# k loaded as plain float32 and rounded on chip by VectorE and GpSimd in turns, outputs planned nine slots behind instead of ten

## The chip, the cores and the metric

One core of one Trainium2 chip runs the whole problem. The metric is device time in microseconds (us), the median of several runs. The profile is one further execution, recorded by the hardware profiler; its span runs from the first to the last instruction of the core.

## The reference, cut to what matters

The inputs are `k` and `v`, each 16 x 2048 x 256 float32 (33.55 MB each), and two vectors `w` and `u` of 256. The output has the shape of `v`. For each batch row and each of the 256 channels a recurrence runs over 2048 time steps:

```python
for t in range(seq_len):
    ww = u + k[b, t]
    qq = max(pp, ww); e1 = exp(pp - qq); e2 = exp(ww - qq)
    out[b, t] = (e1 * aa + e2 * v[b, t]) / (e1 * bb + e2 + 1e-08)
    ww = pp - w + k[b, t]
    qq = max(ww, k[b, t]); e1 = exp(ww - qq); e2 = exp(k[b, t] - qq)
    aa = e1 * aa + e2 * v[b, t];  bb = e1 * bb + e2;  pp = qq
```

So each output is a quotient of two sums over the past with exponentially decaying weights: a numerator with v and a denominator without.

## The kernel before, in words

Time is cut into 16 chunks of 128 steps, and the 16 batch rows into groups of four. One group of one chunk is a slot, n = 0 to 63, and four slots make a chunk (c = n // 4). A tile of k or v for one slot is 128 time steps (on the partitions) x 4 batch rows x 256 channels, 512 KB. In each slot:

- `load_k` and `load_v` bring the two tiles in. For slots 0 to 3 SP issues them (lines 81 and 88), later GpSimd (POOL in the profile; lines 84 and 88). The tile that TensorE multiplies is of type float32r. POOL's load of k has a float32r tile as its target, so the transfer itself converts; SP's loads bring float32 into buffers of v's pool, and `round_k` (VectorE, line 168) copies them into float32r tiles, for the first four slots alone.
- `logs` (TensorE, lines 174 and 177) turns k into two sets of exponents by matrix products, in two PSUM tiles X that are shared with the denominators.
- `exps` (ScalarE, line 181, called ACT) writes their exponentials to the ring `EZR`, which holds 12 slots.
- `cast_v` (line 185) makes a bf16 copy `vb` of v, on VectorE for slots 0 to 9 and on POOL after that; there are two `vb` buffers. `times_v` (VectorE, called DVE, line 190) multiplies it into the ring.
- `sums` (TensorE, line 217) adds up the chunk's totals. After the fourth slot of a chunk a chain of small steps (VectorE lines 223 to 286, two ACT steps at lines 240 and 259, two TensorE steps at lines 230 and 281) computes what the chunk inherits from all earlier ones, and `inject` (four SP transfers of 8 KB, line 295) writes that into the ring.
- `den` and `num` (TensorE, line 307), `log_den` and `inverse` (ACT, lines 316 and 320: a logarithm and an exponential that make the reciprocal), `mult` (VectorE, line 328) and `store` (SP, three transfers at lines 334 and 337) make the output. `num` has one PSUM buffer, the output tile `ot` three buffers, so the product of slot n waits until the store of slot n - 3 has landed.

The order of all this is made by a planner at the end of the kernel. Each piece is a step with an engine, a cost, steps that it must follow, a due time, and a buffer that it takes or gives back. The planner runs these through a list scheduler with a slot of 3.9 us and prints each engine's instructions in the order it finds; on the chip each engine works through its list in that order and waits where an input or a buffer isn't ready. The due time of the output steps of slot n is LAG = 10 slots after that of its exponentials. Where the plan leaves TensorE idle, `zeros` (line 114) inserts multiplications of zeros. Below, a step is named with its slot or chunk: RK for `round_k`, CV for `cast_v`, TV for `times_v`, X for `exps`, LN and INV for the two ACT steps of the output, MUL for `mult`, ST for `store`, IN for `inject`, FR for the first VectorE step of the chain behind line 240.

There are eight buffers of k (`kpool`, NK) and eight of v (`vpool`, NV). A buffer of k comes free when `logs` has read it.

Of the kernel before, what the change touches and what calls it, by code (L numbers as in the profile page):

```python
# [7 lines left out]
F32 = mybir.dt.float32  # L8
F32R = mybir.dt.float32r
# [6 lines left out]
def kernel(  # L16
# [9 lines left out]
    K = tc.keep_in_program_order  # L26
    PE, DVE, SC, POOL, SP = nc.tensor, nc.vector, nc.scalar, nc.gpsimd, nc.sync

    B, T, Dm = k.shape
# [3 lines left out]
    D = 2 * Dm  # L33
    NP = 4 * NST
    RING = 12
    LAG = 10
    BYSP = 4
    EARLY = 10
    NK, NV, NVB, NRD, NOT = 8, 8, 2, 2, 3
    RS = 2.0 ** -20  # L40
    CAP = 54.0
    BIG = 1e30
    SLOT = 3.9
# [2 lines left out]

    consts = ctx.enter_context(tc.tile_pool(name="consts", bufs=1))
    kpool = ctx.enter_context(tc.tile_pool(name="kpool", bufs=NK))
    vpool = ctx.enter_context(tc.tile_pool(name="vpool", bufs=NV))
    vbpool = ctx.enter_context(tc.tile_pool(name="vbpool", bufs=NVB))  # L50
    rpool = ctx.enter_context(tc.tile_pool(name="rpool", bufs=NRD))
# [20 lines left out]
    def rows_of(x, n):  # L72
        c, p = divmod(n, 4)
        return x[4 * p:4 * p + 4, c * TC:(c + 1) * TC, :].rearrange("n t d -> t n d")

    KR, VR, VB = {}, {}, {}

    def load_k(n):
        if n < BYSP:
            KR[n] = vpool.tile([128, 4, Dm], F32, tag="vr", name="kf")  # L80
            K(SP.dma_start(out=KR[n], in_=rows_of(k, n)))
        else:
            KR[n] = kpool.tile([128, 4, Dm], F32R, tag="kr", name="kr")
            K(POOL.dma_start(out=KR[n], in_=rows_of(k, n)))  # L84

    def load_v(n):
        vr = vpool.tile([128, 4, Dm], F32, tag="vr", name="vr")
# [5 lines left out]
    def rows_wu(x, g0):  # L93
        K(POOL.dma_start(out=WU[g0::64, :, :], in_=bass.AP(
            tensor=x.tensor, offset=x.offset, ap=[[0, 2], [0, 2], list(x.ap[0])])))

    load_k(0)
    K(SC.preload_act_table_set("natural_log_exp_and_others"))
    Z = consts.tile([128, 192], BF16, tag="Z", name="Z")
# [63 lines left out]

    X = [psx.tile([128, 2, D], F32, tag=f"X{a}", name=f"X{a}") for a in range(2)]

    def round_k(n):
        kr = kpool.tile([128, 4, Dm], F32R, tag="kr", name="kr")
        K(DVE.tensor_copy(kr, KR[n]))
        KR[n] = kr

    def logs(n, q, a):
        km = KR[n].rearrange("p (i n) d -> p i (n d)", i=2)
        for i in range(2):
            K(PE.matmul(X[a][:, i, :], (NLE, NLZ)[q], km[:, i, :], start=True, stop=False, skip_group_check=True))  # L174
        for i in range(2):
            g = 64 * i
            K(PE.matmul(X[a][:, i, :], CO[g:g + 64, q, :], WU[g:g + 64].rearrange("p n d -> p (n d)"),  # L177
                        start=False, stop=True, tile_position=(g, 0), skip_group_check=True))
# [121 lines left out]
    RD, NUM, OT = {}, {}, {}  # L300
# [42 lines left out]
    def step(name, eng, cost, fn, args=(), after=(), behind=(), due=0.0, port=False, take=None, give=(), move=None):  # L343
        ops[name] = dict(eng=eng, cost=cost, fn=fn, args=args, after=after, behind=behind, due=due, port=port,
                         take=take, give=give, move=move)

    for n in range(NP):
        c = n // 4
        t = SLOT * n
        e = LAG * SLOT  # L350
        last = SLOT * (4 * c + 3)
        early = n < BYSP
        q = "SP" if early else "POOL"
        qc = 0.6 if early else 0.76
        if n:
            step(("LK", n), q, qc, load_k, (n,), behind=[("LK", n - 1)], due=t - 14 * SLOT, take=("V", -1 - n) if early else ("K", n), move=0.524)
            step(("LV", n), q, qc, load_v, (n,), behind=[("LV", n - 1)], due=t - 9 * SLOT, take=("V", n), move=0.524)
        else:
            step(("LK", n), "-", 0.0, None, take=("V", -1 - n), move=0.524)
            step(("LV", n), q, qc, load_v, (n,), take=("V", n), move=0.524)  # L360
        if early:
            step(("RK", n), "DVE", 0.65, round_k, (n,), [("LK", n)], due=t - 2 * SLOT, port=True, take=("K", n),
                 give=[("V", -1 - n)])
        src = ("RK", n) if early else ("LK", n)
        for j in range(2):
            step(("L", j, n), "PE", 0.95, logs, (n, j), [src], [("L", 1 - j, n - 1 + j)], t - 1.5 * SLOT, take=("X", (j, n)),
                 give=[("K", n)] if j else [])
            step(("X", j, n), "ACT", 0.91, exps, (n, j), [("L", j, n), ("NUM", n - RING), ("S", n - RING)],
                 [("X", 1 - j, n - 1 + j)], t, give=[("X", (j, n))])
        step(("CV", n), "DVE" if n < EARLY else "POOL", 0.63 if n < EARLY else 1.0, cast_v, (n,), [("LV", n)],  # L370
             [("CV", n - 1)], t, True, ("VB", n), [("V", n)])
        step(("TV", n), "DVE", 1.14, times_v, (n,), [("X", 1, n), ("CV", n)], [("TV", n - 1)], t + 2 * SLOT, True,
             None, [("VB", n)])
        step(("S", n), "PE", 0.34, sums, (n,), [("TV", n)] + ([("CS", c - 1)] if n % 4 == 0 else []), [("S", n - 1)],
             t + 3 * SLOT)
        if n % 4 == 3:
            chain = (("CS", "DVE", 0.34, copy_sums, ("S", n)), ("TU", "PE", 0.45, turn, ("CS", c), ("BK", c - 1)),
                     ("CT", "DVE", 0.27, copy_turn, ("TU", c)), ("SL", "ACT", 0.23, state_logs, ("CT", c)),
                     ("FR", "DVE", 0.53, state_frames, ("SL", c), ("SN", c - 1)),
                     ("OF", "DVE", 0.39, state_offsets, ("FR", c)), ("SW", "ACT", 0.26, state_weights, ("OF", c)),  # L380
                     ("CH", "DVE", 0.95, state_chain, ("SW", c), ("KP", c - 1)),
                     ("SS", "DVE", 0.36, state_spread, ("CH", c)), ("TK", "PE", 0.23, turn_back, ("SS", c)),
                     ("BK", "DVE", 0.2, copy_back, ("TK", c)))
            for name, eng, cost, fn, *after in chain:
                step((name, c), eng, cost, fn, (c,), after, due=last + 1)
            step(("IN", c), "SP", 2.4, inject, (c,), [("BK", c)], due=last - 9, move=0.0)
            if c + 1 < NST:
                step(("SN", c), "DVE", 0.12, state_next, (c,), [("OF", c)], due=last + 2 * SLOT)
                step(("KP", c), "DVE", 0.12, state_keep, (c,), [("CH", c)], due=last + 2 * SLOT)
        step(("DEN", n), "PE", 0.44, den, (n,), [("IN", c)], [("DEN", n - 1)], t + e, take=("X", ("d", n)))  # L390
        step(("LN", n), "ACT", 0.92, log_den, (n,), [("DEN", n)], [("INV", n - 1)], t + e, take=("RD", n),
             give=[("X", ("d", n))])
        step(("INV", n), "ACT", 0.95, inverse, (n,), [("LN", n)], due=t + e)
        step(("NUM", n), "PE", 0.44, num, (n,), [("IN", c), ("TV", n)], [("NUM", n - 1)], t + e + 1, take=("N", n))
        step(("MUL", n), "DVE", 1.14, mult, (n,), [("NUM", n), ("INV", n)], [("MUL", n - 1)], t + e + 2, take=("OT", n),
             give=[("N", n), ("RD", n)])
        step(("ST", n), "SP", 1.8, store, (n,), [("MUL", n)], due=t + e + 4, move=0.524)
        step(("SD", n), "-", 0.0, None, after=[("ST", n)], give=[("OT", n)])
# [8 lines left out]
        elif name[0] in ("DEN", "NUM", "TK"):  # L407
            ops[name]["after"].append("mats")

    free = {"K": NK, "V": NV, "X": 2, "N": 1, "RD": NRD, "OT": NOT, "VB": NVB}  # L410
    free = {x: [(0.0, j) for j in range(m)] for x, m in free.items()}
    at = {"POOL": 5.6, "SP": 1.3, "ACT": 5.0, "DVE": 5.4, "PE": 6.0, "-": 0.0}
    need, users = {}, {}
# [7 lines left out]
    held, port, hbm, out_end = {}, 0.0, 0.0, 0.0  # L421
    while ready:
        best = {}
        for name, t in ready.items():
            o = ops[name]
            t = max(t, at[o["eng"]], port if o["port"] else 0.0)
            if o["take"]:
                if not free[o["take"][0]]:
                    continue
                t = max(t, min(free[o["take"][0]])[0])  # L430
# [5 lines left out]
        t, _, name = min(pick, key=lambda x: x[:2])  # L436
# [5 lines left out]
        if o["port"]:  # L442
            port = end
# [65 lines left out]
```

## Time and profile before

| | |
|---|---|
| runs without profile | 315.66 us median of 3 (315.4 to 323.72) |
| the profiled execution | 318.16 us, of which its span is 316.4 us |
| mean granted TensorE clock | 0.984 |
| busy | PE 284.3, ACT 259.6, DVE 235.7, POOL 158.6 us |
| moved by DMA | 101.66 MB, of it 67.12 MB read from HBM and 33.55 MB written |

PE's busy time holds 43.1 us of the multiplications of zeros. The loads of k and v go through two queues: q1 (issued by SP, and the stores too) and q0 (issued by POOL). Start times of single steps, as "X 16 starts at 67.4 us", are read from the timeline of the engine; the n-th instruction of a group belongs to slot n (X has two instructions for each slot).

### The profile page before, as it was taken

What the parts mean: (1) busy time and instruction counts of PE and PEld (TensorE: products, weight loads), DVE (VectorE), ACT (ScalarE), POOL (GpSimd) and SP (SyncE); (2) the same over time, 40 slices, a digit from 0 to 9 for tenths busy, and PEclk for the clock granted to TensorE, in tenths of its full rate; (3) what the DMA queues carried; (4) which work ended last, traced back from release to release, by engine and by line L of the source; (5) the groups of instructions that cost most, each with busy time, mean ns of one, the idle gap of its engine ahead of it and who ended that gap; (6) DMA issues with size and microseconds to landing.
All of it is one profiled execution on the core that took longest, in us unless ns stands there. A gap on an engine that the chain in (4) does not pass through costs nothing.

```text
span 316.4 us, 6751 instructions
## 1 busy us (share of the span) xinstructions
PE 284.3 (90%) x2524; PEld 134.0 (42%) x2524; DVE 235.7 (74%) x388; ACT 259.6 (82%) x289; POOL 158.6 (50%) x204
## 2 busy tenths in 40 slices
PE   7999797989797989888998989998998999999991
PEld 6444343434343434333443434434343444446560
DVE  5843869999877997686869687776859696978443
ACT  1776567979797989788897989988897999999880
POOL 7738564976287548664663656455564322200000
PEclk9999599999999999999999999999999999999997
DMA  7999999999999999999999999999999954448477
GB/s 242 358 387 400 399 398 391 370 358 365 377 292 368 366 371 355 369 337 374 383 313 385 338 375 344 323 364 365 388 318 383 317 161 138 134 119 241 130 238 218
DMA packets 83586, 101.66 MB, mean 321 GB/s; under 512 B 8280, under 2 KB 75872, under 8 KB 83552
## 3 DMA queue, kind: packets, MB, share of 16 engines
q0 software_dynamic: 40416, 62.93, 64.8%
q1 hardware_dynamic: 43136, 38.29, 39.2%
q8 instruction: 20, 0.33, 0.4%
q14 instruction: 14, 0.11, 0.1%
HBM read 67.12 MB, written 33.55 MB: 318 GB/s over the span
## 4 chain that ended last, share of the span: by engine, by line
DMA 35%; DVE 24%; PE 19%; SPq 8%; ACT 8%; issue 4%; DVEq 0%; POOL 0%
DMA out_dram<-ot 26%; DMA vr<-in_v_dram 7%; PE X L174 6%; DVE ot L328 6%; DVE AB L266 5%; DVE EZR L190 4%; PE X L177 4%; ACT rd L316 3%; ACT rd L320 3%; PE X L307 3%; SPq L337 3%; SPq L295 2%; PE num L307 2%; SPq L334 2%; DMA EZR<-cb 2%
## 5 line engine op out<-in xcount | busy, mean ns | idle before, releaser
L181 ACT ACTIVATE EZR<-X 128x1024 bf16<-128x1024 f32 x128 | 125.2, 1014 | 21.3 <-PE X L177 20.4
L328 DVE TENSOR_TENSOR ot<-num,rd 128x1024 f32<-128x1024 f32 x64 | 78.5, 1227 | 43.3 <-DMA out_dram<-ot 21.7
L185 POOL CAST vb<-vr 128x1024 bf16<-128x1024 f32 x54 | 61.1, 1131 | 69.1 <-DVE EZR L190 69.1
L190 DVE TENSOR_TENSOR EZR<-EZR,vb 128x2048 bf16<-128x2048 bf16 x64 | 79.3, 1248 | 11.4 <-ACT EZR L181 8.7
L316 ACT ACTIVATE rd<-X 128x1024 f32<-128x1024 f32 x64 | 65.5, 1023 | 13.7 <-PE X L307 11.6
L320 ACT ACTIVATE rd<-rd 128x1024 f32<-128x1024 f32 x64 | 67.6, 1056 | 1.6
L177 PE MATMUL X<-WU,CO 64*128 64x512 f32 x256 | 64.2, 498 | 1.4 <-DMA WU<-in_u_dram 1.4
L84 POOL DMA_DIRECT2D kr<-in_k_dram x60 | 46.5, 775 | 30.1 <-PE X L174 23.2
L88 POOL DMA_DIRECT2D vr<-in_v_dram x60 | 45.3, 755 | 15.5 <-issue 5.3
L174 PE MATMUL X<-kr,NLZ 128*128 128x512 f32 x128 | 47.3, 451 | 0.0
L174 PE MATMUL X<-kr,NLE 128*128 128x512 f32 x128 | 47.1, 449 | 0.0
L114 PE MATMUL TURN<-Z 128*128 128x192 bf16 x348 | 43.1, 260 | 3.2 <-DVE cb L286 2.1
L177 PEld LDWEIGHTS X<-WU,CO 64*128 64x128 f32 x256 | 24.1, 184 | 48.8 <-issue 47.0
L114 PEld LDWEIGHTS <-Z 128*128 128x128 bf16 x348 | 28.8, 103 | 19.9 <-issue 18.5
L307 PE MATMUL num<-EZR,LN 64*64 64x512 bf16 x256 | 25.6, 389 | 8.1 <-DVE ot L328 7.5
L217 PE MATMUL TOT<-EZR,OH 128*32 128x256 bf16 x512 | 26.7, 281 | 3.2 <-DVE EZR L190 3.2
L174 PEld LDWEIGHTS X<-kr,NLE 128*128 128x128 f32 x128 | 19.3, 191 | 17.9 <-issue 8.5
L307 PE MATMUL X<-EZR,L 64*64 64x512 bf16 x256 | 26.2, 398 | 0.3
L174 PEld LDWEIGHTS X<-kr,NLZ 128*128 128x128 f32 x128 | 19.3, 190 | 16.8 <-issue 12.3
L307 PE MATMUL X<-EZR,Id 64*64 64x512 bf16 x256 | 25.0, 376 | 0.0
L307 PE MATMUL num<-EZR,IdN 64*64 64x512 bf16 x256 | 25.0, 376 | 0.0
L266 DVE TENSOR_TENSOR_SCAN AB<-G,TB 128x96 f32<-128x96 f32 x32 | 20.0, 663 | 0.6
(60 smaller groups left out, 166.9 us busy)
## 6 DMA issues: line engine op xcount, KB each, us to landing
kr<-in_k_dram POOLq DMA_DIRECT2D x60, 512.0 KB, 8.6
vr<-in_v_dram POOLq DMA_DIRECT2D x60, 512.0 KB, 8.8
out_dram<-ot SPq DMA_DIRECT2D x64, 256.0 KB, 6.4
out_dram<-ot SPq DMA_DIRECT2D x128, 128.0 KB, 7.0
kf<-in_k_dram SPq DMA_DIRECT2D x4, 512.0 KB, 5.4
vr<-in_v_dram SPq DMA_DIRECT2D x4, 512.0 KB, 9.3
EZR<-cb SPq DMA_DIRECT2D x64, 8.0 KB, 5.1
WU<-in_w_dram POOLq DMA_DIRECT2D x1, 4.0 KB, 5.4
```

The source lines that it names most:

```text
L84: K(POOL.dma_start(out=KR[n], in_=rows_of(k, n)))
L88: K((SP if n < BYSP else POOL).dma_start(out=vr, in_=rows_of(v, n)))
L114: K(PE.matmul(TURN[:, 320:512], Z[:, 0:128], Z, start=True, stop=True, skip_group_check=True))
L174: K(PE.matmul(X[a][:, i, :], (NLE, NLZ)[q], km[:, i, :], start=True, stop=False, skip_group_check=True))
L177: K(PE.matmul(X[a][:, i, :], CO[g:g + 64, q, :], WU[g:g + 64].rearrange("p n d -> p (n d)"), start=False, stop=True, tile_position=(g, 0), ...
L181: K(SC.activation(ez(n)[:, q], X[a], ACT.Exp))
L185: K((DVE if n < EARLY else POOL).tensor_copy(vb, VR.pop(n)))
L190: K(DVE.tensor_mul(ez(n)[:, 2:4], ez(n)[:, 0:2], vb.unsqueeze(1).broadcast_to([128, 2, 2, D])))
L307: K(PE.matmul(out_tile[o:o + HS, i, :], mats[names[s]][r:r + HS, r:r + HS], ez(n)[r:r + HS, q0 + s, i, :], start=s == 0, stop=s == 1, tile ...
L316: K(SC.activation(rd, X[a], ACT.Ln, scale=RS))
L320: K(SC.activation(RD[n], RD[n], ACT.Exp, scale=-1.0))
L328: K(DVE.tensor_mul(o.rearrange("p (i n) d -> p i (n d)", i=2), NUM.pop(n), RD.pop(n)))
```

## The change

All loads of k bring plain float32 into `kpool`, the first four from SP and the others from POOL. Each of the 64 tiles is then rounded into a float32r tile of a new pool `kmpool` with two buffers: on VectorE for slots 0 to 9 and then for the even slots, on POOL for the odd ones. A buffer of k comes free when the rounding has read it, one of `kmpool` when `logs` has read it. The pools of k and v have seven buffers instead of eight, and the first four tiles of k no longer sit in v's pool. LAG is 9 instead of 10. VectorE gets 33 roundings more (37 instead of 4), POOL 27.

```diff
-    LAG = 10
+    LAG = 9
-    NK, NV, NVB, NRD, NOT = 8, 8, 2, 2, 3
+    NK, NKM, NV, NVB, NRD, NOT = 7, 2, 7, 2, 2, 3
+    kmpool = ctx.enter_context(tc.tile_pool(name="kmpool", bufs=NKM))
...
     def load_k(n):
-        if n < BYSP:
-            KR[n] = vpool.tile([128, 4, Dm], F32, tag="vr", name="kf")
-            K(SP.dma_start(out=KR[n], in_=rows_of(k, n)))
-        else:
-            KR[n] = kpool.tile([128, 4, Dm], F32R, tag="kr", name="kr")
-            K(POOL.dma_start(out=KR[n], in_=rows_of(k, n)))
+        KR[n] = kpool.tile([128, 4, Dm], F32, tag="kr", name="kr")
+        K((SP if n < BYSP else POOL).dma_start(out=KR[n], in_=rows_of(k, n)))
...
+    def by_dve(n):
+        return n < EARLY or n % 2 == 0
+
     def round_k(n):
-        kr = kpool.tile([128, 4, Dm], F32R, tag="kr", name="kr")
-        K(DVE.tensor_copy(kr, KR[n]))
-        KR[n] = kr
+        km = kmpool.tile([128, 4, Dm], F32R, tag="km", name="km")
+        K((DVE if by_dve(n) else POOL).tensor_copy(km, KR.pop(n)))
+        KM[n] = km
...
-        if early:
-            step(("RK", n), "DVE", 0.65, round_k, (n,), [("LK", n)], due=t - 2 * SLOT, port=True, take=("K", n),
-                 give=[("V", -1 - n)])
-        src = ("RK", n) if early else ("LK", n)
+        step(("RK", n), "DVE" if by_dve(n) else "POOL", 0.58 if by_dve(n) else 1.0, round_k, (n,), [("LK", n)], [("RK", n - 1)], t - 2 * SLOT, True, ("KM", n), [("K", n)])
         for j in range(2):
-            step(("L", j, n), "PE", 0.95, logs, (n, j), [src], [("L", 1 - j, n - 1 + j)], t - 1.5 * SLOT, take=("X", (j, n)),
-                 give=[("K", n)] if j else [])
+            step(("L", j, n), "PE", 0.95, logs, (n, j), [("RK", n)], [("L", 1 - j, n - 1 + j)], t - 1.5 * SLOT, take=("X", (j, n)),
+                 give=[("KM", n)] if j else [])
```

Since the planner weighs all steps anew, the lists of all engines change. In the steady state VectorE's list goes MUL, RK, TV, MUL where it went TV, MUL; POOL's goes CV, load of v, RK, load of k in the odd slots. On SP, IN of chunk 10 stands between the stores of slots 35 and 36, where it stood between those of 33 and 34. After IN of the last chunk SP has seven stores to issue instead of eight.

More of the change, by code (lines that the diff above doesn't have):

```diff
@@ L74, in rows_of @@
         return x[4 * p:4 * p + 4, c * TC:(c + 1) * TC, :].rearrange("n t d -> t n d")
-    KR, VR, VB = {}, {}, {}
+    KR, KM, VR, VB = {}, {}, {}, {}
     def load_k(n):
-        if n < BYSP:
-            KR[n] = vpool.tile([128, 4, Dm], F32, tag="vr", name="kf")
-            K(SP.dma_start(out=KR[n], in_=rows_of(k, n)))
-        else:
-            KR[n] = kpool.tile([128, 4, Dm], F32R, tag="kr", name="kr")
-            K(POOL.dma_start(out=KR[n], in_=rows_of(k, n)))
+        KR[n] = kpool.tile([128, 4, Dm], F32, tag="kr", name="kr")
+        K((SP if n < BYSP else POOL).dma_start(out=KR[n], in_=rows_of(k, n)))
     def load_v(n):
@@ L164 @@
     X = [psx.tile([128, 2, D], F32, tag=f"X{a}", name=f"X{a}") for a in range(2)]
+    def by_dve(n):
+        return n < EARLY or n % 2 == 0
     def round_k(n):
-        kr = kpool.tile([128, 4, Dm], F32R, tag="kr", name="kr")
-        K(DVE.tensor_copy(kr, KR[n]))
-        KR[n] = kr
+        km = kmpool.tile([128, 4, Dm], F32R, tag="km", name="km")
+        K((DVE if by_dve(n) else POOL).tensor_copy(km, KR.pop(n)))
+        KM[n] = km
     def logs(n, q, a):
-        km = KR[n].rearrange("p (i n) d -> p i (n d)", i=2)
+        km = KM[n].rearrange("p (i n) d -> p i (n d)", i=2)
         for i in range(2):
@@ L355 @@
         if n:
-            step(("LK", n), q, qc, load_k, (n,), behind=[("LK", n - 1)], due=t - 14 * SLOT, take=("V", -1 - n) if early else ("K", n), move=0.524)
+            step(("LK", n), q, qc, load_k, (n,), behind=[("LK", n - 1)], due=t - 14 * SLOT, take=("K", n), move=0.524)
             step(("LV", n), q, qc, load_v, (n,), behind=[("LV", n - 1)], due=t - 9 * SLOT, take=("V", n), move=0.524)
         else:
-            step(("LK", n), "-", 0.0, None, take=("V", -1 - n), move=0.524)
+            step(("LK", n), "-", 0.0, None, take=("K", n), move=0.524)
             step(("LV", n), q, qc, load_v, (n,), take=("V", n), move=0.524)
-        if early:
-            step(("RK", n), "DVE", 0.65, round_k, (n,), [("LK", n)], due=t - 2 * SLOT, port=True, take=("K", n),
-                 give=[("V", -1 - n)])
-        src = ("RK", n) if early else ("LK", n)
+        step(("RK", n), "DVE" if by_dve(n) else "POOL", 0.58 if by_dve(n) else 1.0, round_k, (n,), [("LK", n)], [("RK", n - 1)], t - 2 * SLOT, True, ("KM", n), [("K", n)])
         for j in range(2):
-            step(("L", j, n), "PE", 0.95, logs, (n, j), [src], [("L", 1 - j, n - 1 + j)], t - 1.5 * SLOT, take=("X", (j, n)),
-                 give=[("K", n)] if j else [])
+            step(("L", j, n), "PE", 0.95, logs, (n, j), [("RK", n)], [("L", 1 - j, n - 1 + j)], t - 1.5 * SLOT, take=("X", (j, n)),
+                 give=[("KM", n)] if j else [])
             step(("X", j, n), "ACT", 0.91, exps, (n, j), [("L", j, n), ("NUM", n - RING), ("S", n - RING)],
@@ L408 @@
             ops[name]["after"].append("mats")
-    free = {"K": NK, "V": NV, "X": 2, "N": 1, "RD": NRD, "OT": NOT, "VB": NVB}
+    free = {"K": NK, "KM": NKM, "V": NV, "X": 2, "N": 1, "RD": NRD, "OT": NOT, "VB": NVB}
     free = {x: [(0.0, j) for j in range(m)] for x, m in free.items()}
```

## The prediction

> **What bounds the kernel now.** I read the page's second part first (DMA nearly full until 255 us, then not), next the windows, to price each kind of traffic, then the waits, and last the chain, for the pace by chunk.
>
> ```profile
> DMA  7999999999999999999999999999999954448477
> q0 software_dynamic: 40416, 62.93, 64.8%
> q1 hardware_dynamic: 43136, 38.29, 39.2%
> ```
> The transfers are saturated while loads run. Loads end at 252 us (k of slot 63), and 64 us remain. The windows' columns end with PE clock, DMA share and GB/s:
>
> ```profile
> 11.50:17.00 5.50, 5.49 (x35) 2.36 (x34) 3.88 (x4) 4.73 (x6) 2.72 (x4) 1.00 1.25 340
> 18.50:20.50 2.00, 1.49 (x8) 0.58 (x7) 1.98 (x2) 1.72 (x2) 1.03 (x2) 1.00 1.49 395
> 25.50:27.30 1.80, 1.80 (x9) 0.73 (x7) 1.22 (x2) 1.01 (x2) 1.46 (x2) 1.00 1.05 404
> ...
> 180.00:198.00 18.00, 16.88 (x157) 7.34 (x149) 13.55 (x23) 16.22 (x20) 10.09 (x13) 1.00 1.16 360
> ...
> 252.00:270.00 18.00, 17.84 (x165) 8.22 (x157) 14.81 (x24) 17.23 (x20) 4.21 (x5) 1.00 0.56 172
> ```
> Line 1: k from POOL beside v from SP. Line 2: k alone. Line 3: v alone from POOL. The packet records say why they differ: POOL's k, converted on the way, moves as 1 KB packets of 61 ns (30,728 of them); POOL's v, read through the same slicing but not converted, as 4 KB packets of 159 ns (7,680). The last line is after the loads: ACT is 96% busy, at 360 GB/s it was 90%.
>
> ```profile
> DVE ot L328 <- DMA out_dram<-ot: 21.7, 12, 3.2
> POOL vb L185 <- DVE EZR L190: 69.1, 34, 3.5
> POOL kr L84 <- PE X L174: 23.2, 12, 5.7
> ```
> Nobody waits long for loaded k or v: k of slot 40 lands at 150.1 us and X 40 starts at 178.1. What waits is MUL, on its store (line 1), and the list behind it. The chain shows one such round per chunk:
>
> ```profile
> 147.65 1.23 DVE ot L328
> ...
> 165.54 1.23 DVE ot L328
> ...
> 254.07 1.23 DVE ot L328
> ...
> 270.69 1.23 DVE ot L328
> ```
> 17.9 us per chunk under loads, 16.6 after them. Stores land late for the full DMA:
>
> ```profile
> out_dram<-ot SPq DMA_DIRECT2D x29, 256.0 KB, 7.3
> ...
> out_dram<-ot SPq DMA_DIRECT2D x10, 256.0 KB, 2.4
> ```
> (126 to 252 us; 255 to 290 us). So: bound by DMA throughput, felt through the stores and three `ot` buffers; ACT's pace, 4.15 us a slot, is the floor below.
>
> **The change part by part.** The sum is made on the profiled execution, span 316.4 us (318.16 with what lies around it; the median is 315.66). I take the same difference off the median. X 12 starts at 48.3, X 56 at 250.0: 44 slots, 4.58 us each.
>
> *k without conversion.* k becomes traffic of v's kind. I cut 20 to 251 us into bins of 1 us, left out those with packets of IN, and fitted bin length to MB moved: 2.70 us per MB of k, 2.51 of v, 2.84 of stores. With a term for k and stores moving together: stores 2.67 alone. Per slot (0.524 MB each) the change saves 0.524 x (2.70 - 2.51) = 0.10 on k and 0.524 x (2.84 - 2.67) = 0.09 on stores, 0.19 us; x 44 slots = -8.4. This is a rate gain, so it counts as long as the DMA stays full and the pace above 4.15 (4.58 - 0.19 = 4.39 does). Ends: solo rates only (395 to 404 GB/s) give 0.03 a slot, -1.3; a DMA that no longer bounds gives 4.15, 44 x 0.43 = -18.9. On the other side, v's large packets take more of the DMA than k's: in the microsecond from 144.5 us v moved 328 KB and stores 34, while at 11.5 to 17 us k and SP's tiles shared evenly. Stores may land later still. The nearest row is X 16 to X 20, where stores took 9 to 11 us: 4.82 a slot, 44 x 0.24 = +10.6. I take the fit, which includes both kinds of stretches. Before X 12: 0.94 MB of k moved beside 0.93 MB from SP at 340 GB/s; at the 382 of SP's tiles alone (4 to 10 us), 5.5 us shrink by 0.6.
>
> *33 roundings more on VectorE.* The four rows of line 168 last 0.63 to 0.99 us, mean 0.77: 25 us in all, 1.5 per chunk. In the steady chunk VectorE is busy 13.55/18 x 17.9 = 13.5 us; 15.0 of 17 still fits, with the waits for stores (about 2) as the cover. So in the steady state 0; if that cover goes, 11 chunks x 1.5 = +17. MUL now stands ahead of RK in VectorE's list, so a late store also delays RK and, behind it, TensorE's `logs` and ACT's X; `num` was already held by MUL before (18 us of waits), so I add nothing. At the start there is no cover: RK 8 and RK 9 stand behind FR 0, which waited until 30.2 us for POOL's memsets. X 9 started at 36.0; RK 9 now comes after FR's group, SN, RK 8, TV 4, CH 0, two casts and BK (31.4 + 0.8 + 1.2 + 1.4 + 1.6 + 1, about 38 us), then 1.3 us of TensorE: X 9 near 39. +3.0 (0 if POOL's faster loads bring its memsets forward by 3; +5 if RK 10, 12, 14 and 16 also find VectorE full, as from 54 to 72 us, 17.07 of 18).
>
> *27 roundings on POOL.* Nearest row: the cast of line 185, 1.13 us mean: 0.57 per slot more. POOL works 10.1 of 18 us; it waits 69.1 us for VectorE, which hides 30. Behind RK in its list stand the loads and the next CV; loads are some 25 us ahead. 0; if the cover goes, that is the rival below.
>
> *DMA issue beside VectorE's copies.* POOL's issue of k lasts 752 ns in the median, 1202 at most, that one under a rounding of 0.99 us: at most 33 x 0.45 = 15 us of POOL, under the same 69.1. 0.
> [...]
>
> *Buffers.* Seven of k instead of eight, but freed by RK and with two behind; seven of v. Landing takes 8.6 to 8.8 us of a 30 us cycle: 0; the stretch in which POOL waited for k's buffers (23.2 us, mostly before 80 us) bounds a loss at +1 slot, 4.6.
>
> *LAG 9.* One LN and INV (1.02 + 1.06) stand ahead of the last X. ACT sat idle for 21 us before 54 us and takes some of it: +1.0 (0 to +2.1). After the last IN SP issues seven stores instead of eight, which came 2.0 us apart (297.06 to 304.99, four steps): -2.0 (0 if ACT sets the end). IN loses slack: IN 7 landed near 161, LN 28 started at 176; minus two slots, 6 remain.
>
> Sum: 316.4 - 8.4 - 0.6 + 3.0 + 1.0 - 2.0 = 309.4 span, -7.0; median 308.7.
>
> **Rivals.** *A, ACT becomes the bound* (store waits vanish): 44 x -0.43 = -18.9, -0.6 + 3.0 + 1.0 - 2.0: -17.5, and with VectorE's 15 of 16.6 leaving some wait, half of the extra gain: -12.3, 303.4. For it: 16.6 us per chunk without loads. Against: the fit leaves the DMA near full.
>
> *B, VectorE takes the gain back.* Where a POOL cast overlapped a TV fully, TV took 1.66 us on average instead of 1.22 (four cases), and a scan of line 266 1.21 instead of 0.34 (twelve). Two POOL roundings per chunk, one on each: +1.3; 13.5 + 1.5 + 1.3 = 16.3 and store waits of 1.3 give 17.6, 4.40 instead of the 4.48 of the chain: -3.5 - 0.6 + 3.0 + 1.0 - 2.0 = -2.1, 313.6.
>
> *C, k's packets stay as they are* (the conversion isn't what makes them 1 KB): nothing gained, +2.0: 317.7. Against: v has the same slicing and 4 KB packets.
>
> *D, slower: VectorE and POOL serialise and VectorE becomes the bound.*
>
> ```profile
> 59.98 1.88 DVE L190 TENSOR_TENSOR EZR<-EZR,vb 128x2048 bf16<-128x2048 bf16 x1
> ...
> 60.66 2.09 POOL L185 CAST vb<-vr 128x1024 bf16<-128x1024 f32 x1
> ```
> 1.22 and 1.04 us alone, about 2.8 together. Before, CV waits for the TV that frees `vb` and so falls beside MUL, which it doesn't slow (1.22); a POOL rounding waits only for TensorE's read and can fall anywhere. If all four roundings of a chunk collide, two on scans (+0.87) and two on casts (+1.04): +3.8, VectorE 13.5 + 1.5 + 3.8 = 18.8 per chunk, 4.70: 44 x 0.22 = +9.7, +1.4 for the rest: 326.8. It decides from +3.0 per chunk on (18.0, above the chunk of 17.9); I expect 0.5 to 1.5.
> [...]
>
> **How the numbers follow.** Forecast 0.40 (own range 304 to 313), A 0.16, B 0.20, C 0.04, D 0.20. Two per cent, about what a measurement of this kernel can tell from no change, is 6.3 us: faster is below 309.3, slower above 322. The forecast lies at the edge: 0.27 faster, 0.13 within. Faster: 0.27 + 0.16 = 0.43. Within: 0.13 + 0.17 of B + 0.04 = 0.34. Slower: 0.20 + 0.03 of B = 0.23. The range reaches from inside A to inside D, 301 to 323, leaving about 0.04 below and 0.15 above. Predicted: 308.7.
>
> **What would show it.** Right: k's packets on q0 of 4 KB; the chain's MUL rounds at 17 to 17.3 us under loads; stores landing at 6 to 7; X 9 at 38 to 40; TV at 1.22. Wrong: TV and scans lengthened throughout (D, B), rounds at 16.6 with no wait on stores (A), or stores landing later than 7.5 us behind v-like packets, which would break the first step.

## The result, and the profile after

The changed kernel takes 349.26 us (median of 4 runs, 345.7 to 351.13), the kernel before took 315.53 us on the same chip (4 runs). The ratio is 1.104, with a 95% interval of 1.0924 to 1.1156. It is slower; 308.7 us was predicted, with a range to 323. The profiled execution took 345.7 us, with a span of 344.0 us and a mean granted clock of 0.905 (before 318.16, 316.4 and 0.984).

Start times of the exponentials divide the difference of the spans. "Pace" below is the time from X 16 to X 56 divided by 40 slots.

| stretch (us) | before | after | difference |
|---|---|---|---|
| start to X 16 | 67.4 | 85.2 | +17.7 |
| X 16 to X 56 | 182.6 (pace 4.57) | 194.2 (pace 4.86) | +11.6 |
| X 56 to X 63 | 29.4 | 30.1 | +0.7 |
| X 63 to the end | 37.0 | 34.5 | -2.4 |

Executions of one kernel differ by up to 5% here, with more or fewer stretches at half clock (the profiles of e1, e4, e5 and e15 are of slow ones, those of e7 and e14 of the fastest by some 2%), so profiles are compared stretch by stretch, with the medians beside them.

From the page of after, the granted clock, the DMA's busy share, and the two queues:

```profile
PEclk9965559999987999789998999699996999999997
DMA  8999758999998999989999999999998997164677
...
q0 software_dynamic: 17376, 62.93, 54.3%
q1 hardware_dynamic: 43136, 38.29, 34.0%
```

The same bytes move on q0 in 17,376 packets instead of 40,416: k now moves in 4 KB packets, as the first step of the prediction had it. But the clock is at half from the third to the sixth slice and dips in every fourth or fifth slice from the twelfth on. DMA issues from 126 to 252 us, with the time to landing last:

```profile
kr<-in_k_dram POOLq DMA_DIRECT2D x27, 512.0 KB, 6.7
out_dram<-ot SPq DMA_DIRECT2D x27, 256.0 KB, 6.0
```

Stores land in 6.0 us instead of 7.3. The window (PE, PEld, DVE, ACT, POOL busy, clock, DMA share, GB/s) that was shown of before:

```profile
180.00:198.00 18.00, 16.92 (x137) 7.32 (x140) 15.20 (x25) 13.78 (x16) 10.96 (x13) 0.91 1.00 327
```

The DMA moves less (327 instead of 360 GB/s), ACT does less in the same time (13.78 us, before 16.22), and VectorE, at 15.20 of 18, isn't full. So I look for a wait. The waits (total, times, longest):

```profile
POOL kr L81 <- DVE km L168: 62.2, 23, 5.1
ACT EZR L181 <- PE X L177: 54.4, 31, 9.8
...
DVE ot L328 <- ACT rd L320: 19.5, 15, 3.3
POOL vb L185 <- DVE EZR L190: 16.1, 7, 5.6
...
PE TURN L281 <- DVE CB L271: 8.5, 4, 2.2
```

The same waits of ACT and TensorE before:

```profile
ACT EZR L181 <- PE X L177: 20.4, 17, 6.6
...
PE TURN L281 <- DVE CB L271: 5.9, 10, 1.0
```

The wait of MUL on its store, 21.7 us before, is gone. ACT now waits 54.4 us for TensorE (20.4 before). In the last line TensorE waits for the state's chain on VectorE: before it did so ten times, for up to 1.0 us; now it does so four times, for 2.0 to 2.2 us each. A fifth wait of this length goes to the same place, and they return every eight slots. The timeline of after around the chain of chunk 3 (start, duration, then the instruction):

```profile
97.68 1.05 POOL L185 CAST vb<-vr 128x1024 bf16<-128x1024 f32 x1
97.69 1.20 DVE L263 TENSOR_TENSOR TB<-TS,G 128x128 f32<-128x128 f32 x1
...
98.92 2.13 DVE L266 TENSOR_TENSOR_SCAN AB<-G,TB 128x96 f32<-128x96 f32 x2
...
99.78 1.05 POOL L168 CAST km<-kr 128x1024 fp32r<-128x1024 f32 x1
101.08 0.45 DVE L271 TENSOR_TENSOR CB<-AB,G 128x128 bf16<-128x128 f32 x1
...
101.33 1.67 DVE L276 COPY TB<-AB 128x64 f32<-128x64 f32 x1
...
101.59 0.61 PE L281 MATMUL TURN<-Id,CB 128*128 128x128 bf16 x4 [2.04 <-DVE CB L271]
101.88 1.05 POOL L185 CAST vb<-vr 128x1024 bf16<-128x1024 f32 x1
101.95 1.20 PE L174 MATMUL X<-km,NLE 128*128 128x512 f32 x2
...
104.05 0.27 DVE L286 CAST cb<-TURN 128x128 bf16<-128x128 f32 x1
```

Three casts of GpSimd, the middle one the rounding of slot 21, follow each other beside the chain. The product of line 263 takes 1.20 us (0.28 where nothing is beside it), the two scans 2.13 (0.61 where nothing is beside them), the copy of line 276 1.67 (0.24). TensorE stands idle for 2.04 us; the copy holds up MUL and behind it the last step of the chain (line 286), which starts 2.46 us after the turn-back of line 281. TensorE's next products take 1.20 us instead of 0.74: the granted clock is 0.5 from 101.3 us on for 6.8 us. The same happens with the roundings of slots 29, 37, 45 and 53 (idle 2.15 us each time, half clock for 3.4 or 6.8 us), but beside slot 37 the copy of line 276 stays short and the last step of the chain isn't held.

Such meetings aren't new in themselves. VectorE's scans of line 266, before and then after:

```profile
L266 DVE TENSOR_TENSOR_SCAN AB<-G,TB 128x96 f32<-128x96 f32 x32 | 20.0, 663 | 0.6
```

```profile
L266 DVE TENSOR_TENSOR_SCAN AB<-G,TB 128x96 f32<-128x96 f32 x32 | 18.8, 630 | 0.6
```

They cost VectorE no more in all. Before, the two scans took 1.3 us in most chunks, beside a cast of v, and TensorE then waited mostly 0.7 us; after, they take 0.61 in one chunk and 2.13 in the next.

The start is lost in another place. TensorE's timeline of after:

```profile
16.81 0.28 PE L217 MATMUL TOT<-EZR,OH 128*32 128x256 bf16 x2
18.89 0.40 PE L217 MATMUL TOT<-EZR,OH 128*32 128x256 bf16 x6 [1.79 <-DVE EZR L190]
19.22 2.46 PE L111 MATMUL TURN<-Z 128*128 128x192 bf16 x15
21.61 0.40 PE L217 MATMUL TOT<-EZR,OH 128*32 128x256 bf16 x2
25.13 0.61 PE L217 MATMUL TOT<-EZR,OH 128*32 128x256 bf16 x6 [3.12 <-DVE EZR L190]
25.82 1.19 PE L174 MATMUL X<-km,NLE 128*128 128x512 f32 x2
```

Line 217 adds up slots 1 and 2 and waits for their products with v. `logs` of slot 4 stand behind them, so X 4 starts at 27.8 instead of 18.7 us. v is late: the tile of slot 3 lands at 23.2 us instead of 18.4. By the packet records, from 13 to 15 us SP's queue, with v in 1 KB packets, moved 170 KB in after, and GpSimd's queue, now in 4 KB packets, 640; before it was 333 and 331. From 19.4 us on the clock is at half for 30.7 us. So of the 17.7 us up to X 16, 9.1 are there at X 4, and X 4 to X 16 takes 57.4 us instead of 48.7.

### The profile page after: what moved, and what is told of

The parts are those of the page before. It is cut to its first block, busy times and chain, and to the rows that moved or that the text cites. A ratio compares the mean times of both kernels' runs of the same rounds, so it can differ in the third digit from the quotient of the medians.

```text
span 344.0 us, 6785 instructions
## 1 busy us (share of the span) xinstructions
PE 304.3 (88%) x2520; PEld 142.3 (41%) x2520; DVE 274.3 (80%) x421; ACT 261.1 (76%) x289; POOL 188.0 (55%) x231
## 3 DMA queue, kind: packets, MB, share of 16 engines
q0 software_dynamic: 17376, 62.93, 54.3%
## 5 line engine op out<-in xcount | busy, mean ns | idle before, releaser
L181 ACT ACTIVATE EZR<-X 128x1024 bf16<-128x1024 f32 x128 | 126.9, 1018 | 55.6 <-PE X L177 54.4
L190 DVE TENSOR_TENSOR EZR<-EZR,vb 128x2048 bf16<-128x2048 bf16 x64 | 89.3, 1404 | 0.0
L81 POOL DMA_DIRECT2D kr<-in_k_dram x60 | 45.8, 764 | 71.1 <-DVE km L168 62.2
L177 PE MATMUL X<-WU,CO 64*128 64x512 f32 x256 | 68.9, 535 | 1.4 <-DMA WU<-in_u_dram 1.4
L174 PE MATMUL X<-km,NLZ 128*128 128x512 f32 x128 | 51.4, 486 | 0.0
L174 PE MATMUL X<-km,NLE 128*128 128x512 f32 x128 | 50.9, 482 | 0.4
L307 PE MATMUL num<-EZR,LN 64*64 64x512 bf16 x256 | 27.9, 417 | 9.4 <-DVE ot L328 7.6
L168 POOL CAST km<-kr 128x1024 fp32r<-128x1024 f32 x27 | 28.4, 1053 | 7.1 <-PE X L174 4.4
L174 PEld LDWEIGHTS X<-km,NLZ 128*128 128x128 f32 x128 | 21.1, 207 | 19.7 <-issue 11.5
L168 DVE CAST km<-kr 128x1024 fp32r<-128x1024 f32 x37 | 25.3, 684 | 4.2 <-PE X L174 4.1
L174 PEld LDWEIGHTS X<-km,NLE 128*128 128x128 f32 x128 | 21.0, 206 | 17.0 <-issue 13.5
L307 PE MATMUL num<-EZR,IdN 64*64 64x512 bf16 x256 | 27.2, 404 | 0.0
```

Of the source, the lines that this page charges most:

```text
L168: K((DVE if by_dve(n) else POOL).tensor_copy(km, KR.pop(n)))
L181: K(SC.activation(ez(n)[:, q], X[a], ACT.Exp))
L190: K(DVE.tensor_mul(ez(n)[:, 2:4], ez(n)[:, 0:2], vb.unsqueeze(1).broadcast_to([128, 2, 2, D])))
L307: K(PE.matmul(out_tile[o:o + HS, i, :], mats[names[s]][r:r + HS, r:r + HS], ez(n)[r:r + HS, q0 + s, i, :], start=s == 0, stop=s == 1, tile ...
```

## The experiments

"After" in a diff is the changed kernel. "Thin" means that a rounding copies 8 of 1024 columns: the rest of k is left out, while transfers, waits and lists stay. Theory 1: the roundings hold VectorE and the chain, and the start is a separate loss by v's late tiles. Rivals stand with each run.

**e1, every rounding thin** (two fixed float32r tiles in place of the pool).

```diff
-        K((DVE if by_dve(n) else POOL).tensor_copy(km, KR.pop(n)))
+        K((DVE if by_dve(n) else POOL).tensor_copy(km[:, :, 0:2], KR.pop(n)[:, :, 0:2]))
```

> The changed kernel with its own lists of steps, but each rounding copies only 8 of a tile's 1024 columns into one of two fixed float32r tiles (the rest of k is left out of the products; the loads, waits and order stay). It leaves the plain loads and the order and takes the rounding work away. Theory 1 (VectorE is the bound through the roundings, 22 us of work, and through collisions with POOL's casts, about 16 us more; the slow start is a matter of its own): the pace from X 16 to X 56 falls from 4.86 us a slot to about 4.4, the start still loses about 9 us between X 3 and X 4, and the time is 320 to 328 us. Theory 2 (the order, with outputs nine slots behind, costs the time, not the work): 340 us or more. Theory 3 (the loads as such cost it): 340 us or more, with waits on loads.

328.59 us (322.61 to 332.41; before 319.1 on that chip). The pace is 4.41, 0.15 under that of before: without the roundings' data most of the forecast gain of 0.19 is there. The start is worse, X 16 at 90.9: k's tiles come free sooner, GpSimd's loads of k go out up to 1.2 us earlier, and v's tile 3 lands at 28.9 us.

**e2, all roundings on VectorE** (the lists are planned anew).

```diff
-        return n < EARLY or n % 2 == 0
+        return True
```

> The changed kernel with all roundings on VectorE, none on POOL. Theory 1a (VectorE's own work is the bound): 27 x 0.68 = 18 us more for VectorE, less the collisions that POOL's roundings caused (5 to 10 us): 348 to 360 us. Theory 1b (the collisions with POOL's roundings are most of the loss): 330 to 340 us. Theory 2 (order): no forecast, near 349.

343.55 us, ratio 1.0778 (1.0668 to 1.0888); pace 4.72. Between the two forecasts, and with other lists: it decides nothing alone.

**e3, after with LAG 10**, and **e4, before with LAG 9** (one number each).

```diff
-    LAG = 9
+    LAG = 10
```

```diff
-    LAG = 10
+    LAG = 9
```

> The changed kernel with outputs planned ten slots behind, as before. Theory 1: 345 to 353 us, since the work and the collisions stay. Theory 2 (nine slots cost the time): below 330 us.

> The kernel before with outputs planned nine slots behind, nothing else changed. Theory 1: 312 to 319 us, the lag alone is worth about nothing. Theory 2: above 330 us.

e3: 358.76 us, ratio 1.1296 (1.1208 to 1.1385), pace 4.96. Slower than both theories had it: LAG 9 isn't what made the changed kernel slow. Up to chunk 11 no scan of e3 took over 1.1 us, and its pace is slower than that of after: other lists lose as much in other places, and what is said of the scans below holds for the lists of after. e4: 321.62 us, ratio 1.0094 (1.0041 to 1.0147): X 16 at 76.2, pace 4.60, 34.2 us after X 63. So LAG 9 alone costs some 3 us, inside 2%: it takes 2.8 off the end and puts more ahead of X 16 (17 us of half clock among it, 6.8 before).

**e5, k of slots 4 to 15 converted by the transfer**, as before (lists planned anew), and **e6, the same with thin roundings from slot 16 on** (into the two fixed tiles of e1).

```diff
-        KR[n] = kpool.tile([128, 4, Dm], F32, tag="kr", name="kr")
+        KR[n] = kpool.tile([128, 4, Dm], F32R if conv(n) else F32, tag="kr", name="kr")
...
+        if not conv(n):
             step(("RK", n), ...
```

> The changed kernel, but k of slots 4 to 15 is loaded with conversion as before (1 KB packets on GpSimd's queue, no rounding); slots 16 and up as changed. Theory 1 (two separate losses: the start, by v's tile 3 kept waiting beside k's 4 KB packets, some 14 to 17 us of the time; and the roundings in the steady part, some 12 us): the exponential of slot 16 starts at 68 to 72 us instead of 85.0, the pace from X 16 to X 56 stays near the 4.85 us of the changed kernel, the time is 331 to 337 us. Rival (the start's loss is only moved: a kernel that starts earlier waits for its loads or its state later): X 16 near 70, but the pace over 5.0 and the time over 340.

> As the run with k of slots 4 to 15 loaded with conversion, and from slot 16 on each rounding copies only 8 of 1024 columns into one of two fixed tiles (the rest of k is left out of the computation there, all transfers, waits and every engine's list stay). If start and roundings together are the whole loss, what is left is the gain that was forecast, fewer packets and nine slots: X 16 at 68 to 72 us, a pace of 4.40 to 4.45, and 303 to 311 us, faster than the kernel before. If something else of the change costs (the seven buffers, k's transfers starting after v's), over 316.

e5: 344.06 us (334.69 to 344.22), X 16 at 74.9, pace 5.05: near the rival's numbers. e6: 324.17 us, ratio 1.0196 (1.0085 to 1.0307), X 16 at 71.5, pace 4.63. Theory 1 missed both times, and e6 came out on the side of its rival (something else costs, the seven buffers or the order of the transfers). New lists and an earlier start stand in the way of a reading: with the same thin roundings the pace was 4.41 in e1 and is 4.63 here. The runs below keep the lists of after, but for e8; none changes the buffers alone.

**e7, 23 idle matmuls ahead of five turn-backs**.

```diff
         CT = TURN[:, 192:320]
+        if c in (3, 5, 7, 9, 11):
+            zeros(23)
```

> The changed kernel with 23 idle matmuls (about 2 us) on TensorE ahead of the turn back of chunks 3, 5, 7, 9 and 11, where TensorE stood idle 2.0 to 2.2 us and its granted clock then was 0.5 for 3.4 to 6.8 us. Theory A (the half clock is a good part of the steady loss): those stretches of half clock go or get shorter, and with them 1 to 3 us at each of the five places: 334 to 344 us, pace from X 16 to X 56 4.60 to 4.75. Theory B (the half clock follows from VectorE being late and costs little of its own): pace 4.82 to 4.95, 346 to 353 us.

341.69 us (335.18 to 345.22): the time is theory A's, the pace of 4.76 lies between the two. After, then e7, from 90 to 280 us (clock third from the end):

```profile
90.00:280.00 190.00, 171.08 (x1428) 73.51 (x1420) 165.82 (x237) 157.95 (x177) 123.17 (x137) 0.92 0.97 326
```

```profile
90.00:280.00 190.00, 174.21 (x1576) 80.10 (x1576) 175.88 (x241) 161.82 (x181) 124.92 (x137) 1.00 0.98 332
```

With the idle stretches filled, the half clock is gone from the steady part, and 0.10 us a slot comes back, 4.0 us of the 17.7 (0.443 x 40) that separate after from e1. By chance this run also had only 6.8 us of half clock in the start, where nothing was changed: 51.0 us from X 4 to X 16, in after 57.4.

**e8, odd slots converted, even ones rounded by VectorE**, slots 4 to 15 converted (lists planned anew).

```diff
+    def conv(n):
+        return 4 <= n and (n < 16 or n % 2 == 1)
...
```

> k of slots 4 to 15 and of every odd slot after them loaded with conversion; even slots from 16 on loaded plain and rounded by VectorE; GpSimd rounds nothing. It halves the gain in the packets and leaves VectorE 24 roundings after the start. By a line between the pace without roundings (4.41) and the one with all of them on VectorE (4.72), 4.5 to 4.6: 312 to 320 us, no different from the kernel before to within 2%. If the cost is GpSimd's own roundings against VectorE and VectorE's own are hidden, a pace of 4.45 to 4.5 and 308 to 312.

327.21 us, ratio 1.0352 (1.0279 to 1.0425); X 16 at 72.0, pace 4.67. Slower than either forecast.

**e9, the lists of after, k of slots 4 to 15 converted**, their roundings left out of the lists.

```diff
-        KR[n] = kpool.tile([128, 4, Dm], F32, tag="kr", name="kr")
+        KR[n] = kpool.tile([128, 4, Dm], F32R if 4 <= n < 16 else F32, tag="kr", name="kr")
...
     def round_k(n):
+        if 4 <= n < 16:
+            KM[n] = KR.pop(n)
+            return
```

> The changed kernel with its own lists on every engine, except that k of slots 4 to 15 is loaded with conversion (1 KB packets) and its roundings are left out. Theory 1 (the start was lost because v's tiles 2 and 3, on SP's queue in 1 KB packets, wait beside k's 4 KB packets): v's tile 3 lands at 18 to 20 us instead of 23.0, the exponential of slot 4 starts at 18.5 to 21 instead of 27.6, that of slot 16 at 68 to 75 instead of 85.0; the pace from 16 to 56 stays 4.8 to 4.95; 330 to 338 us. Rival (the order of the lists, sums of slot 2 ahead of the logarithms of slot 4, and the half clock behind it): slot 4 at 24 us or later, slot 16 over 78, and over 341 us.

338.27 us, ratio 1.0607 (1.048 to 1.0733). v's tile 3 lands at 17.8 us, X 4 starts at 21.3, X 16 at 75.5, pace 4.90. Theory 1 holds for the landing and for X 4 within 0.3 us: with 1 KB packets of k the start is 9.7 us shorter, though the sums of slot 2 stand ahead of `logs` of slot 4 as in after. What was forecast for X 16 and the time was missed by 0.5 and 0.3 us. The roundings of slots 4 to 15 are gone here too, but they aren't what held the start: e1, with thin roundings and 4 KB packets, has tile 3 at 28.9 us.

**e10, only VectorE's roundings thin**, and **e11, only GpSimd's**.

```diff
...
+        w = 2 if by_dve(n) else Dm
+        K((DVE if by_dve(n) else POOL).tensor_copy(km[:, :, 0:w], KR.pop(n)[:, :, 0:w]))
```

(e11 with `not by_dve(n)`; both with the two fixed tiles of e1.)

> The changed kernel with its own lists; VectorE's 37 roundings copy 8 of 1024 columns (the rest of k is left out there), GpSimd's 27 stay whole. The pace from X 16 to X 56 was 4.86 with all roundings whole and 4.41 with none. Theory 1 (VectorE's own work is the larger part): 4.45 to 4.60. Rival (GpSimd's casts beside VectorE's instructions are the larger part): 4.65 to 4.80. Read by the pace, since the start moves by itself.

> The counterpart: GpSimd's 27 roundings copy 8 of 1024 columns, VectorE's 37 stay whole. Theory 1 (VectorE's own work is the larger part): a pace of 4.65 to 4.80. Rival (GpSimd's casts beside VectorE are the larger part): 4.45 to 4.60. If both halves add up, the two paces lie together about 0.45 us over twice 4.41.

e10: 345.84 us, pace 4.73. e11: 332.66 us, pace 4.49. Theory 1, in the form that VectorE's own work is the larger part, falls, and the rival is right in both. Over 4.41, VectorE's 37 roundings cost 0.07 us a slot, GpSimd's 27 cost 0.32 (40 x 0.32 = 13 us). The scans of line 266 in after, here lines 269, e10 first, then e11:

```profile
L269 DVE TENSOR_TENSOR_SCAN AB<-G,TB 128x96 f32<-128x96 f32 x32 | 18.8, 630 | 0.6
```

```profile
L269 DVE TENSOR_TENSOR_SCAN AB<-G,TB 128x96 f32<-128x96 f32 x32 | 10.4, 367 | 0.6
```

The products with v are slow in both (1304 and 1385 ns mean, after 1404), and at e11's pace that is hidden. The scans are what differs: new theory, the cost lies in the five roundings beside them.

**e12, zeros in the start too** (20 and 40 ahead of the sums of slots 1 and 2, beside those of e7).

```diff
         t = TOT
+        if n in (1, 2):
+            zeros(20 * n)
```

> The kernel with 23 idle matmuls ahead of the turn back of five chunks, and 20 and 40 more ahead of the sums of slots 1 and 2, where TensorE waited 1.8 and 3.1 us in the changed kernel before some 31 us at half clock. Theory A (that half clock costs about 6 us of the start: the run with zeros in the five gaps alone started with 7 us of it, by chance, and had X 16 at 78.9 instead of 85.0): no half clock over 7 us before X 16, X 16 at 76 to 80, and a time of 331 to 337 us in every run. Theory B (the clock isn't set by this gap): 31 us of half clock again, X 16 at 83 or later, 340 us or more.

339.16 us (335.49 to 345.1). No half clock before 76.5 us; X 12 at 55.2 (after 62.8), X 16 at 80.3, just over theory A's range, in a new 6.8 us of half clock. The half clock of the start was worth 6.3 us (e7) to 7.6 up to X 12; the total was forecast 2 us too low.

**e13, only the five roundings thin**, and **e14, three thin copies in place of each**.

```diff
...
+        five = n in (21, 29, 37, 45, 53)
+        w = 2 if five else Dm
+        kr = KR.pop(n)
+        for j in range(3 if five else 1):
+            K((DVE if by_dve(n) else POOL).tensor_copy(km[:, :, j * w:j * w + w], kr[:, :, j * w:j * w + w]))
```

(e13 with one copy in place of three; both with the two fixed tiles of e1.)

> The changed kernel with its own lists; only GpSimd's roundings of slots 21, 29, 37, 45 and 53 copy 8 of 1024 columns (the rest of k is left out in those slots), the other 22 of GpSimd and all 37 of VectorE are whole. Theory 1 (the cost lies in these five, beside the scans of the state's chain): the scans of chunks 3, 5, 7, 9 and 11 take about 0.35 us instead of 1.86, TensorE's idle 2 us and the half clock behind it go, pace from X 16 to X 56 4.50 to 4.60 instead of 4.86. Rival (all 27 cost alike): 5 of 27 of 0.37, a pace of 4.76 to 4.82.

> As the run with five thin roundings, but each of the five is three small copies of 8 columns, which keep GpSimd for about as long (0.4 us each by the thin roundings' mean) with 1/40 of the data. Theory 1 (what costs is the data that GpSimd moves beside VectorE's float32 scan): the pace of the thin run, 4.50 to 4.60. Rival (what costs is GpSimd's time in its list, the cast of v and the loads behind it): 4.70 to 4.90.

e13: 337.92 us, ratio 1.0667 (1.0557 to 1.0776), with X 16 at 91.5 and a pace of 4.45: lower than forecast. By this run 5 of 64 roundings carry 0.41 of 0.44 us a slot, 16 us. The shares of e10, e11 and e13 don't add up to better than 0.1 a slot (all 27 of GpSimd's carry 0.32 by e10, 0.37 by after less e11), with one profile of each. The chain of chunk 5 in e13:

```profile
140.16 1.05 POOL L191 CAST vb<-vr 128x1024 bf16<-128x1024 f32 x1
140.17 1.20 DVE L269 TENSOR_TENSOR TB<-TS,G 128x128 f32<-128x128 f32 x1
...
141.40 0.61 DVE L272 TENSOR_TENSOR_SCAN AB<-G,TB 128x96 f32<-128x96 f32 x2
...
142.04 0.44 DVE L277 TENSOR_TENSOR CB<-AB,G 128x128 bf16<-128x128 f32 x1
142.27 0.27 POOL L174 CAST km<-kr 128x8 fp32r<-128x8 f32 x1
142.29 0.23 DVE L282 COPY TB<-AB 128x64 f32<-128x64 f32 x1
...
142.54 0.40 PE L287 MATMUL TURN<-Id,CB 128*128 128x128 bf16 x4 [0.63 <-DVE TB L282]
...
143.53 0.28 DVE L292 CAST cb<-TURN 128x128 bf16<-128x128 f32 x1
```

The first cast still slows line 269's product to 1.20 us, but the scans take 0.61, TensorE waits 0.63 us instead of 2.04, the last step (line 292) follows 0.99 us after the turn-back instead of 2.46, and there is no half clock from 95.2 us to X 56. e14: 337.52 us, pace 4.47, but its three copies kept GpSimd for 0.45 us together, not for the 1.05 of a whole rounding. So it doesn't tell data from time, and that stays open. It does answer another rival, that a late start makes the pace after it look good: X 16 comes at 83.3 us in e14, ahead of after, and X 56 at 262.3 instead of 279.4.

**e15, the five on VectorE** at the same place of the order (whole computation), and **e16, that (and slot 61) with e9's start**.

```diff
-        K((DVE if by_dve(n) else POOL).tensor_copy(km, KR.pop(n)))
+        K((DVE if by_dve(n) or n in (21, 29, 37, 45, 53) else POOL).tensor_copy(km, KR.pop(n)))
```

> The changed kernel with its own lists; the roundings of slots 21, 29, 37, 45 and 53 are issued on VectorE at the same place of the order (the whole computation is done). Theory 1: the collision goes and VectorE gets 0.69 us more in eight slots: pace 4.55 to 4.68, and a time 7 to 12 us under that of the changed kernel, 337 to 343. Rival: VectorE, which then waits itself for the tile that the rounding writes to, holds the chain as long: pace over 4.75, 344 or more.

> The run with k of slots 4 to 15 converted (338.3 us), and GpSimd's roundings of slots 21, 29, 37, 45, 53 and 61 on VectorE too. If the two losses add up: X 16 at 73 to 77 us, pace 4.55 to 4.68, 324 to 331 us, still slower than the kernel before. If they are one: over 333.

e15: 340.53 us (329.01 to 345.17), pace 4.70 (4.61 from X 24 on): the median as theory 1 had it, the pace just over. In e15 the scans are at 0.61 again, TensorE waits 0.6 to 1.0 us, and the chain's last step follows 1.6 us after the turn-back (1.0 in e13): VectorE's own rounding now stands there. e16: 338.64 us, ratio 1.0532 (1.0379 to 1.0684), X 16 at 78.6, pace 4.68: not the sum of the two, and over 333 us, as forecast for the case that the two are one loss. The rounding of slot 17, still GpSimd's, stood beside the scan of chunk 2 (1.86 us).

**e17, slots 4 to 15, 17, 21, 29, 37, 45, 53 and 61 converted by the transfer** (lists of after, whole computation; the tiles of slots 11 and 15 come from `kmpool`).

```diff
+    def conv(n):
+        return 4 <= n < 16 or n in (17, 21, 29, 37, 45, 53, 61)
...
```

> The changed kernel with its own lists; k of slots 4 to 15, and of slots 17, 21, 29, 37, 45, 53 and 61, is loaded with conversion as before and not rounded (the tiles of slots 11 and 15 come from the pool of rounded tiles, so that k's loads wait less); the whole computation is done. Theory 1 (start and the roundings beside the scans are separate losses, and with both gone what was forecast is left): X 16 at 69 to 75 us, no scan of 1.86 us in chunks 3 to 13, a pace of 4.43 to 4.55, a time of 314 to 321 us, within 2% of the kernel before. Rival (the scans' place is taken by other collisions once the order in time shifts): a pace over 4.65 and 325 us or more.

331.97 us, ratio 1.0456 (1.0395 to 1.0516). X 16 at 72.9, no scan over 1.1 us, and in chunks 5, 7 and 9 the chain is as short as in e13 (2.1 us from scan to last step): so far theory 1. But the pace is 4.80, the rival's. From e17's timeline:

```profile
121.16 1.23 DVE L337 TENSOR_TENSOR ot<-num,rd 128x1024 f32<-128x1024 f32 x1 [2.19 <-DMA out_dram<-ot]
...
132.11 0.75 POOL L87 DMA_DIRECT2D kr<-in_k_dram  x1 [4.71 <-DVE km L177]
132.86 1.05 POOL L194 CAST vb<-vr 128x1024 bf16<-128x1024 f32 x1
133.94 1.23 DVE L199 TENSOR_TENSOR EZR<-EZR,vb 128x2048 bf16<-128x2048 bf16 x1 [2.12 <-POOL vb L194]
```

GpSimd waits 4.71 us to issue a load of k whose tile VectorE's rounding has to free, the cast of v stands behind it in GpSimd's list, and VectorE's product waits 2.12 us for that cast; MUL waits for its store again (12.4 us from 100 to 270 us). That these waits set e17's pace is read from the timeline, not tested. So both causes are shown, each by itself (e9, e13), and e13 by leaving data of k out; that mending both gives back their sum was forecast in e6, e16 and e17 and missed each time. No version here beats the kernel before.

## Why the prediction was wrong, step by step

- **k without conversion, -0.19 us a slot: borne out, with some luck in the size.** With no rounding in the way the pace is 4.41 in e1, 0.19 under e4 (LAG 9 too) and 0.15 under before. The lists differ, so the agreement to 0.01 is luck. Stores landed in 6.0 us, as the forecast had it.
- **27 roundings on GpSimd, 0: the step that failed.** It counted GpSimd's time (28.4 us under 69.1 of waits) and that was right and beside the point. In place of 0 the runs show 0.32 us a slot, 13 us (e10), or up to 16 (e13), nearly all of it in five roundings that stand beside the chain. Rival B priced one collision on a product with v and one on a scan by their length, +1.3 us of VectorE's busy time per chunk; D asked for 3.0 per chunk to fill VectorE, and its +1.04 for two casts beside each other stands in no timeline of before or after: in after none of VectorE's 37 roundings overlapped a cast of GpSimd by more than 0.06 us, and they lasted 0.63 to 0.78 us. VectorE didn't fill (15.20 of 18), and its scans took no more in all than before. What the pace shows is the chain's own lateness where another engine waits for it: the turn-back came 1.4 to 1.5 us later than in e13 (2.04 - 0.63), and in four of the five the chain's last step another 1.4 to 1.5 (2.46 - 0.99), 13 us together. With the 4.0 us for the half clock behind them (e7) that is an estimate of 17 us, beside the 16 that e13 measured. Of the rivals, D had the side and the engines right, not the way.
- **33 roundings on VectorE, 0 in the steady state: nearly right**, 0.07 a slot, 3 us (e11).
- **The start, +3.0 for RK 8 and RK 9: wrong cause and size.** X 9 was forecast near 39 and came at 51.4 us, X 16 came 17.7 us later. 9.7 of that goes when k of slots 4 to 15 keeps its 1 KB packets (e9); the half clock behind the wait for v makes up some 6 to 7 of it (e7, e12). The two shares overlap, since e9 had 10.2 us of half clock up to X 16 and after 30.7. The prediction named what was needed, that large packets took more of the DMA than small ones (328 KB of v against 34 KB of stores in one microsecond of before), but applied it to the stores alone and kept the even share of the old packets for v's first tiles. By the packet records from 13 to 15 us, SP's queue got 170 of 810 KB, 21%, in 1 KB packets beside 4 KB ones, and 50% before, with 1 KB packets on both queues. What divides the DMA so, no run here shows.
- **LAG 9, +1.0 and -2.0: the end right (-2.4; e4 -2.8), the rest mis-sized.** Together they cost about +3 in e4, not -1.
- **DMA issue and buffers, 0:** neither shows as a cost in the traces of after, where from slot 11 on k's tiles land 19 us and more ahead of their roundings, for all of GpSimd's 62.2 us of waits; no run tests the buffers alone. One reading was wrong: the issue of 1202 ns stood beside a cast of v (line 185, from 12.49 us), not beside a rounding. Those beside roundings lasted 0.76 to 1.03 us, at most 0.28 over the median, so the bound was smaller still. In e17 a wait of this kind did come to bear, since a cast stood behind it.
- **The signs named beforehand:** packets of 4 KB and stores landing in 6.0 us came as said. MUL's rounds under loads lasted some 19 us instead of 17 to 17.3, and TV 1.40 us on average instead of 1.22, the sign of B and D. But TV was at 1.53 in e13, where the pace is 4.45, so the longer products with v aren't what sets it.

How a cast of GpSimd lengthens an instruction of VectorE stays open. The product of line 263 took 1.20 us beside a cast of 1.05 and 0.28 with none beside it. The scan ended 0.2 us behind the rounding (101.05 and 100.83 us), but it grew by 1.5 us, more than the rounding's 1.05, so a wait of one cast's length doesn't give all of it. MUL took 1.21 us on average beside 13 casts that overlapped it by 0.8 us or more, and 1.22 with none beside it.

## What to carry to other kernels

When work moves to GpSimd, look up which VectorE instruction of a latency chain will stand beside it, and price what that chain releases, not busy time: by e13, 5 casts of 64 cost here more than the other 59. When one stream's packets grow, look at what shares the DMA with it in small packets and is needed first: here v's tile 3 landed at 23.2 us instead of 18.4. And test a part with every engine's list held fixed: replanned lists, with an earlier start, moved the pace by 0.22 us a slot (e6 against e1).

## What the runs showed of the hardware

- In after, 2.0 to 2.2 us in which TensorE did nothing came with a granted clock of 0.5 for 3.4 or 6.8 us, which began between 0.3 us ahead of their end and 2.5 us behind it, five times of five. In the start it was 30.7 us, behind 1.79 us of idleness and with 3.12 us more inside (34.1 in e1 and e13). These lengths are 1, 2, 9 and 10 times 3.4 us. With idle matmuls in that place it didn't come (e7: a clock of 1.00 from 90 to 280 us, in after 0.92). The length of the idleness alone doesn't decide: in e12, with the same matmuls, 1.25 us of it from 98.9 us on was followed by 3.4 us at half clock, and in e15, after 2.35 us of it from 118.1 us on, the clock stayed full until 125.9.
- Equal instruction lists in the start differ by chance with it: from X 4 to X 16 60.7 us in e13, 26.6 of them at half clock, and 52.0 in e14, 7.9 at half clock.
- Two VectorE instructions of after, which at their length elsewhere would have ended up to 0.3 us ahead of the recorded start of a GpSimd cast, ended 0.1 to 0.2 us behind that cast (the second scan above would have ended near 99.5 us, the rounding is recorded from 99.78; the copy of line 276 would have ended near 101.6, the cast is recorded from 101.88). Why, no run shows.
